# The mixer's pooled input: one matmul block over all 256 tokens with the channels on partitions, mapped in one go, and the output product started with the pooled channels

## The chip, the cores and the metric

The kernel runs on one core of a Trainium2 chip. The metric is the device time of one execution in microseconds (us); smaller is better. PE is TensorE (matmul), ACT is ScalarE, DVE is VectorE, POOL is GpSimd, SP is the engine whose queue issues the DMAs. The array of PE and its weight load overlap.

## What is computed

Two layers, each: a SwiGLU feed-forward part (FFN), a mixer, a second FFN, each followed by a residual sum and a layer norm. 256 tokens, 1024 channels. The mixer projects the input to 2560 channels: 512 for pooling (u) and 4 x 512 for a gated recurrence with four heads (q, f, v, g). The reference, cut to the pooling branch and the mixer's end:

```python
def multiscale_pool(u, pool_w, pool_scale):          # windows 2, 4, 8, 16 for four groups of 128 channels
    c = jnp.cumsum(u32, axis=1)
    for g, w in enumerate(POOL_WINDOWS):
        ...
        cnt = jnp.minimum(pos + 1, w)
        means.append((cg - lag) / cnt)
    pooled = jnp.stack(means, axis=2) - u32
    y = jnp.einsum('bsgc,gcd->bsgd', pooled, pool_w)
    return y.reshape(B, S, D_POOL) * pool_scale
...
h = x @ w_in[l]
y_pool = multiscale_pool(u, pool_w[l], pool_scale[l])
y_hgrn = head_rms_norm(hgrn2_recurrence(q, f_raw, v, lb), hgrn_norm_g[l]) * silu(g)
mix = concatenate([y_pool, y_hgrn]) @ w_out[l]
x = layer_norm(ALPHA * x + mix, ln_g[l, 1], ln_b[l, 1])
```

## The kernel before

**Numbers and products.** Every factor of a large product is split into a rounded part and its rest (`halves`, line 101: an ACT cast writes the high part, a DVE subtraction the low part), and a product is three matmuls (`mm3`, lines 95 to 99: high x high, high x low, low x high). In the projections of the mixer the stationary operand is a 128x128 piece of the transposed input `xt` and the moving one 512 columns of a weight. One `mm3` is one **slot**: it calls `later.tick()`, and work that was queued with `later(n, fn)` is written into the program n slots further on. PE's order is the order of this writing; ACT, DVE, POOL and SP take an order that a scheduler makes from priorities.

**Weights.** All weights come through one stream of 512 KB pieces (`Weight`, line 107): a DMA on SP's queue into one of five `raw` buffers, an ACT cast to `wh`, a DVE subtraction to `wl` (both at lines 102 and 103, 128x1024 elements), into a ring of eight pairs. A `raw` buffer is free for the next DMA when DVE's subtraction has read it; a pair in the ring is free when PE has made its last use of it (`used`).

**The mixer** (line 520) runs five projection blocks of 512 channels, each for two halves of 128 tokens, eight slots a half: f and q, then v, g and u. Each block has four weight pieces. Between the slots stand the decays (L634), the Gram matrices of the recurrence (L681, L686: `grams`), their product across the halves (L705, `cross`), the outputs per half (L722, L724: `output`), which DVE and POOL normalise into `y`, and the transposes of `y` (L740), eight slots after the outputs. u is made per half with the tokens on partitions: ACT copies it (L752), five slots later four transposes bring the channels onto partitions (L765), ACT copies them into `sum1` (L767), DVE makes the running sums for the windows (L773, L776, L777), nine slots later four matmuls apply `pool_w` (L783), and ACT and DVE scale and split the result into the operand of the output product (L787, L788). These matmuls with `pool_w` and those of the recurrence are full fp32, which PE runs as two passes, each with an instruction of its own.

**The output product** follows: for each half 16 slots over the eight pieces of `w_out`, in the order of `WOUT_ORDER`, which puts the recurrence's four pieces first. After a half comes its layer norm (lines 243 to 251 on DVE), and its transposes (L177) stand in the next half or the next FFN. The freed ring takes the first weights of that FFN.

Of the kernel before, what the change touches and what calls it, by code (L numbers as in the profile page):

```python
# [10 lines left out]
F32 = mybir.dt.float32  # L11
F32R = mybir.dt.float32r
U8 = mybir.dt.uint8
AF = mybir.ActivationFunctionType
# [17 lines left out]
M32, M8, S32 = 0, 96, 192  # L32
WINDOWS = (2, 4, 8, 16)
PAD = 16
WOUT_ORDER = (4, 5, 6, 7, 0, 1, 2, 3)
TINY = 2.0 ** -60
NEG = -1e30
RAW, NW, NX, ND = 5, 8, 2, 6
AHEAD, BEHIND = 100, 400
PINNED, STARTED = 4, 4  # L40
HT = 6
WARM = 17


# [30 lines left out]
def trunk(ctx: ExitStack, tc: tile.TileContext, t, out: bass.AP):  # L75
# [434 lines left out]
    class Mixer:  # L510
        def __init__(self, l):
            self.l = l
            self.win = [[Weight(t["win"][l, b, kq], "w", NW) for kq in range(4)] for b in range(NB)]
            self.wout = {kt: Weight(t["wout"][l, kt], "w", NW) for kt in WOUT_ORDER}

        def run(self):
            return mixer(self.l, self.win, self.wout)
# [1 line left out]
    def mixer(l, win, wout):  # L519
# [14 lines left out]
        def mixed(hf):  # L534

            if hf:
                mt[hf] = xth[:, place[0]], xtl[:, place[0]]
            else:
                mt[hf] = [xtp.tile([P, KT, P], F32R, name=n) for n in ("mth", "mtl")]
            return mt[hf]  # L540
# [177 lines left out]
        def output(hf):  # L718
            po = psa.tile([P, NH, P], F32, name="acc")
            for h in range(NH):  # L720
                hs = slice(h * P, (h + 1) * P)
                nc.tensor.matmul(po[:, h, :], Pm[hf][:, h, :], v[hf][:, hs], start=True, stop=hf == 0)  # L722
                if hf == 1:
                    nc.tensor.matmul(po[:, h, :], P01[0][:, h, :], v[0][:, hs], start=False, stop=True)  # L724
            sq = mp.tile([P, NH, P], F32, name="tB", bufs=2)
            nc.scalar.activation(sq, po, AF.Square)
            ms = sp.tile([P, NH], F32, name="ms")
            nc.vector.tensor_reduce(ms, sq, mybir.AxisListType.X, ALU.add)
            nc.vector.tensor_scalar(ms, ms, 1.0 / P, RMS_EPS, ALU.mult, ALU.add)
            nc.gpsimd.tensor_tensor(ms, ms, neghalf, ALU.pow)  # L730
            y = mp.tile([P, NH, P], F32, name="y", bufs=2)
            for h in range(NH):
                nc.vector.scalar_tensor_tensor(y[:, h, :], po[:, h, :], ms[:, h:h + 1],
                                               sg[hf][:, h * P:(h + 1) * P], ALU.mult, ALU.mult)

            def go():
                mixed(hf)
                pt = psg.tile([P, NH * P], F32, name="gu").rearrange("p (k t) -> p k t", k=NH)
                for h in range(NH):
                    nc.tensor.transpose(pt[:, h, :], y[:, h, :], ident)  # L740
                mh, ml = (m[:, 4:8, :] for m in mt[hf])
                nc.scalar.activation(mh, pt, AF.Copy, scale=gn[:, l:l + 1])
                nc.vector.scalar_tensor_tensor(ml, pt, gn[:, l:l + 1], mh.bitcast(F32), ALU.mult, ALU.subtract)
                ready[hf].add(1)
            later(8, go)

        ready = [set(), set()]
        sums = {}

        def post_u(hf, ps):  # L750
            un = mp.tile([P, 512], F32, name="u")
            nc.scalar.copy(un, ps)  # L752
            if hf == 0:
                for w in (1,) + WINDOWS[:-1]:
                    sums[w] = mp.tile([P, 4 if w < 4 else 6 - w.bit_length(), PAD + P], F32, name=f"sum{w}")

            def pooled():
                for w in sums:
                    if hf == 0:
                        nc.gpsimd.memset(sums[w][:, :, 0:PAD], 0.0)  # L760
                    else:
                        nc.gpsimd.tensor_copy(sums[w][:, :, 0:PAD], sums[w][:, :, P:P + PAD])
                pt = psg.tile([P, 4 * P], F32, name="gu").rearrange("p (k t) -> p k t", k=4)
                for g in range(4):
                    nc.tensor.transpose(pt[:, g, :], un[:, g * P:(g + 1) * P], ident)  # L765
                now = slice(PAD, PAD + P)
                nc.scalar.copy(sums[1][:, :, now], pt)  # L767
                pl = mp.tile([P, 4, P], F32, name="tB", bufs=2)
                for g, w in enumerate(WINDOWS):

                    half = sums[w // 2][:, -(4 - g):, :]
                    dst = sums[w][:, :, now] if w in sums else pl[:, g:g + 1, :]
                    nc.vector.tensor_tensor(dst, half[:, :, now], half[:, :, PAD - w // 2:PAD + P - w // 2], ALU.add)  # L773
                    mean = dst[:, 0, :]
                    if hf == 0:
                        nc.vector.tensor_tensor(mean[:, 0:PAD], mean[:, 0:PAD], fix[:, g, :], ALU.mult)  # L776
                    nc.vector.scalar_tensor_tensor(pl[:, g, :], mean, 1.0 / w, sums[1][:, g, now], ALU.mult, ALU.subtract)  # L777
                later(9, lambda: mapped(pl))

            def mapped(pl):  # L780
                py = psg.tile([P, 4 * P], F32, name="gu").rearrange("p (k t) -> p k t", k=4)
                for g in range(4):
                    nc.tensor.matmul(py[:, g, :], pw[:, g, :], pl[:, g, :], start=True, stop=True)  # L783
                for g in range(4):
                    mh, ml = (m[:, g, :] for m in mt[hf])
                    sc = pscale[:, l, g:g + 1]
                    nc.scalar.activation(mh, py[:, g, :], AF.Copy, scale=sc)  # L787
                    nc.vector.scalar_tensor_tensor(ml, py[:, g, :], sc, mh.bitcast(F32), ALU.mult, ALU.subtract)  # L788
                ready[hf].add(0)
            later(5, pooled)  # L790

        post_f(0, ps_f0)
        post_q(0, block(1, 0))
        post_f(1, block(0, 1))
        post_q(1, block(1, 1))
        for b, post in ((2, post_v), (3, post_g), (4, post_u)):
            for hf in range(2):
                ps = block(b, hf)
                if (b, hf) == (3, 0):
                    tc.keep_in_program_order(nc.scalar.preload_act_table_set("silu_and_others"))  # L800
                post(hf, ps)
        gb = load_gb(l, 1)
        for hf in range(2):
            if hf == 1:
# [1 line left out]
                guard.__exit__(None, None, None)  # L806
                guard = open_ffn()
            accs = [psa.tile([P, 512], F32, name="acc") for _ in range(2)]
            for n, kt in enumerate(WOUT_ORDER):
                later.wait(lambda: kt // 4 in ready[hf])  # L810
                wh, wl = wout[kt].parts
                for c in range(2):
                    cs = slice(c * 512, c * 512 + 512)
                    mm3(accs[c], mt[hf][0][:, kt, :], mt[hf][1][:, kt, :], wh[:, cs], wl[:, cs],
                        n == 0, n == KT - 1)
                wout[kt].used()
            if hf == 0:
                place.reverse()
# [43 lines left out]
def _layout(inputs):  # L862
# [3 lines left out]
        both = np.stack([gate, up], axis=2).reshape(DEPTH, KT // 2, 2, P, 2, NG, GW)  # L866
        return both.transpose(0, 5, 1, 3, 2, 4, 6).reshape(DEPTH, NG, KT // 2, P, ET)

    w_in = a["w_in"].reshape(DEPTH, KT // 2, 2, P, NB, 512)[:, :, :, :, [2, 1, 3, 4, 0]]
    cum, masks, fix = _constants()  # L870

    w0 = gu(a["ffn1_gate"], a["ffn1_up"])[0, 0].reshape(KT // 2, P, 2, 512).transpose(0, 2, 1, 3).reshape(KT, P, 512)
# [35 lines left out]
```

## Time and profile before

| | us |
|---|---|
| median of three runs (958.11 to 958.52) | 958.29 |
| time of the profiled execution | 958.23 |
| its span from first to last instruction | 956.5 |
| PE busy in the span | 946.6 |
| DVE busy | 654.8 |
| ACT busy | 519.6 |
| POOL busy | 32.4 |

Around the span lie 1.7 us. The page of the profile gives for each engine the time in which at least one of its instructions ran. Matmuls overlap on PE, so the duration of one is longer than the step from one start to the next; what a matmul costs is read from steps between starts in the timeline.

### The profile page before, as it was taken

The page shows a single profiled execution, that of the slowest core. Times are in us where ns is not written, and L with a number is a line of the kernel's source. Part 1 is how long each engine was busy: PE and PEld are TensorE (multiplying, and loading weights), DVE is VectorE, ACT ScalarE, POOL GpSimd, SP SyncE. Part 2 cuts the span into 40 slices and gives each one's busy share as a digit, 9 for nine tenths or more (in the row PEclk, how much of TensorE's full clock was granted, in tenths as well). Part 3 has the DMA queues.
Part 4 walks back from the last instruction along what each step waited for, and adds up shares of the span by engine and source line. Part 5 has one row for each costly group of instructions (what it writes and reads, how often), then busy time and mean ns, then how long its engine had stood idle before and what let it go on. Part 6 is the DMA issues. An engine that isn't in the chain of part 4 may idle for free. (4 is left out here: it accounts for less than half of the span.)

```text
span 956.5 us, 13129 instructions
## 1 busy us (share of the span) xinstructions
PE 946.6 (99%) x4817; PEld 800.0 (84%) x4817; DVE 654.8 (68%) x1104; ACT 519.6 (54%) x809; POOL 32.4 (3%) x50
## 2 busy tenths in 40 slices
PE   9999999999999999999999999999999999999996
PEld 7888888888887888888888888888888888888885
DVE  6875656679789765656676565557898896575625
ACT  6765454368456755444445645433985466546420
POOL 0000000001110000000000000000021000000000
PEclk9999999999999999999999999999999999999999
DMA  8977775332627876565346766552327377676301
GB/s 318 336 243 251 254 247 169 109 103 97 219 88 247 311 232 222 191 205 169 123 157 239 237 211 211 174 155 99 110 67 265 112 266 262 222 240 215 114 1 45
DMA packets 50801, 180.22 MB, mean 188 GB/s; under 512 B 6192, under 2 KB 6192, under 8 KB 50736
## 3 DMA queue, kind: packets, MB, share of 16 engines
q1 hardware_dynamic: 50544, 178.85, 55.5%
q8 instruction: 38, 0.62, 0.3%
q0 software_dynamic: 192, 0.53, 0.2%
q14 instruction: 27, 0.22, 0.1%
HBM read 178.30 MB, written 1.05 MB: 188 GB/s over the span
## 5 line engine op out<-in xcount | busy, mean ns | idle before, releaser
L102 ACT CAST wh<-raw 128x1024 fp32r<-128x1024 f32 x196 | 205.1, 1051 | 100.9 <-DMA raw<-in_gu 35.7
L103 DVE TENSOR_TENSOR wl<-raw,wh 128x1024 fp32r<-128x1024 f32 x196 | 235.9, 1219 | 27.0 <-PE gu L300 15.3
L300 PE MATMUL gu<-xt,wh 128*128 128x512 f32 x768 | 180.6, 391 | 0.0
L103 DVE TENSOR_TENSOR dl<-raw,dh 128x1024 fp32r<-128x1024 f32 x88 | 106.5, 1223 | 101.6 <-ACT dh L102 96.0
L300 PEld LDWEIGHTS gu<-xt,wh 128*128 128x128 f32 x768 | 144.1, 188 | 31.7
L102 ACT CAST dh<-raw 128x1024 fp32r<-128x1024 f32 x88 | 91.6, 1049 | 109.7 <-DMA raw<-in_dn 101.3
L96 PE MATMUL acc<-dh,hth 128*128 128x512 f32 x352 | 140.0, 398 | 0.1
L98 PE MATMUL acc<-dh,htl 128*128 128x512 f32 x352 | 138.1, 392 | 0.0
L97 PE MATMUL acc<-dl,hth 128*128 128x512 f32 x352 | 137.4, 390 | 0.0
L96 PE MATMUL gu<-wh,xt 128*128 128x512 f32 x320 | 128.7, 402 | 0.0
L98 PE MATMUL gu<-wh,xt 128*128 128x512 f32 x320 | 125.5, 392 | 0.0
L97 PE MATMUL gu<-wl,xt 128*128 128x512 f32 x320 | 125.0, 391 | 0.0
L300 PE MATMUL gu<-xt,wl 128*128 128x256 f32 x768 | 99.6, 282 | 0.0
L300 PEld LDWEIGHTS gu<-xt,wl 128*128 128x128 f32 x768 | 96.8, 191 | 1.9
L323 DVE TENSOR_TENSOR sil<-gu,sil 128x256 f32<-128x256 f32 x64 | 27.0, 422 | 83.7 <-ACT sil L322 83.7
L98 PEld LDWEIGHTS acc<-dh,htl 128*128 128x128 f32 x352 | 66.0, 188 | 14.8 <-DVE htl L103 0.2
L97 PEld LDWEIGHTS acc<-dl,hth 128*128 128x128 f32 x352 | 66.2, 188 | 12.7 <-DVE dl L103 0.3
L96 PEld LDWEIGHTS acc<-dh,hth 128*128 128x128 f32 x352 | 66.2, 188 | 12.5 <-ACT hth L102 0.5
L98 PEld LDWEIGHTS gu<-wh,xt 128*128 128x128 f32 x320 | 60.1, 188 | 13.1
L97 PEld LDWEIGHTS gu<-wl,xt 128*128 128x128 f32 x320 | 60.2, 188 | 11.4
L96 PEld LDWEIGHTS gu<-wh,xt 128*128 128x128 f32 x320 | 60.1, 188 | 11.0
L300 PE MATMUL gu<-xt,xh 128*128 128x512 f32 x256 | 62.4, 396 | 0.0
(182 smaller groups left out, 1056.2 us busy)
## 6 DMA issues: line engine op xcount, KB each, us to landing
raw<-in_gu SPq DMA_DIRECT2D x172, 512.0 KB, 4.4
raw<-in_dn SPq DMA_DIRECT2D x88, 512.0 KB, 4.6
raw<-in_win SPq DMA_DIRECT2D x40, 512.0 KB, 4.2
raw<-in_wout SPq DMA_DIRECT2D x16, 512.0 KB, 4.2
lng<-in_ln_g SPq DMA_DIRECT2D x6, 512.0 KB, 4.7
lnb<-in_ln_b SPq DMA_DIRECT2D x6, 512.0 KB, 6.0
raw<-in_first SPq DMA_DIRECT2D x5, 384.0 KB, 5.7
x<-in_first SPq DMA_DIRECT2D x3, 384.0 KB, 7.2
```

The source lines that it names most:

```text
L96: nc.tensor.matmul(ps, lh, wh, start=start, stop=False)
L97: nc.tensor.matmul(ps, lh, wl, start=False, stop=False)
L98: nc.tensor.matmul(ps, ll, wh, start=False, stop=stop)
L102: first = nc.scalar.copy(dst_h, src)
L103: return first, nc.vector.tensor_tensor(dst_l, src, dst_h.bitcast(F32), ALU.subtract)
L300: nc.tensor.matmul(ps[i][part][:, 2 * S - w:], weight.parts[lo][:, c:c + P], x[:, 0:w], start=kt == 0 and not lo, stop=kt == KT - 1 and lo ...
L323: nc.vector.tensor_tensor(dst, p[:, 0:S], dst, ALU.add)
```

## The change

The blocks of u and g change places: in the rearranged `w_in` u is now block 3 and g block 4. The projection of u is no longer made per half. `pooled_input` runs it once for all 256 tokens with the weight as the stationary operand (128 channels at a time) and the input as the moving one (256 tokens), so that the channels lie on partitions from the start: 8 x 4 x 3 matmuls of 256 columns; six of them count as a slot. ACT copies the two results into one set of running sums for all tokens, which takes the buffers of the decays (`EA`, `EB`), DVE makes the sums at once, and twelve slots later `mapped` applies `pool_w` to 256 tokens at a time and writes the operands of both halves. The output product takes the pieces of `w_out` in their natural order, the pooled channels first.

```diff
-WOUT_ORDER = (4, 5, 6, 7, 0, 1, 2, 3)
+MAPPED = 12
...
             def go():
-                mixed(hf)
                 pt = psg.tile([P, NH * P], F32, name="gu").rearrange("p (k t) -> p k t", k=NH)
...
-        def post_u(hf, ps):
-            un = mp.tile([P, 512], F32, name="u")
-            nc.scalar.copy(un, ps)
...
+        def pooled_input():
+            ps = [psg.tile([P, 2, S], F32, name="gu") for _ in range(2)]
+            for kt in range(KT):
+                later.wait(lambda: min(xT[0].done, xT[1].done) > kt)
+                weight = win[3][kt // 2]
+                xh, xl = (xt2[:, kt, n].rearrange("p h t -> p (h t)") for n in range(2))
+                for i in range(4):
+                    c = (kt % 2) * 512 + i * P
+                    wh, wl = (part[:, c:c + P] for part in weight.parts)
+                    for n, (w, x) in enumerate(((wh, xh), (wh, xl), (wl, xh))):
+                        nc.tensor.matmul(ps[i // 2][:, i % 2, :], w, x,
+                                         start=kt == 0 and n == 0 and i % 2 == 0,
+                                         stop=kt == KT - 1 and n == 2 and i % 2 == 1)
+                    if i % 2:
+                        later.tick()
+                if kt % 2:
+                    weight.uses = 1
+                    weight.used()
+            sums = {w: mp.tile([P, 4 if w < 4 else 6 - w.bit_length(), PAD + S], F32, name="EA" if w < 4 else "EB", bufs=2)
+                    for w in (1,) + WINDOWS[:-1]}
+            for w in sums:
+                nc.gpsimd.memset(sums[w][:, :, 0:PAD], 0.0)
+            for i, p in enumerate(ps):
+                for hf in range(2):
+                    nc.scalar.copy(sums[1][:, 2 * i:2 * i + 2, PAD + hf * P:PAD + hf * P + P],
+                                   p[:, :, place[hf] * P:place[hf] * P + P])
+            pl = mp.tile([P, 4, S], F32, name="pl")
+            now = slice(PAD, PAD + S)
+            for g, w in enumerate(WINDOWS):
+                half = sums[w // 2][:, -(4 - g):, :]
+                dst = sums[w][:, :, now] if w in sums else pl[:, g:g + 1, :]
+                nc.vector.tensor_tensor(dst, half[:, :, now], half[:, :, PAD - w // 2:PAD + S - w // 2], ALU.add)
+                mean = dst[:, 0, :]
+                nc.vector.tensor_tensor(mean[:, 0:PAD], mean[:, 0:PAD], fix[:, g, :], ALU.mult)
+                nc.vector.scalar_tensor_tensor(pl[:, g, :], mean, 1.0 / w, sums[1][:, g, now], ALU.mult, ALU.subtract)
+            later(MAPPED, lambda: mapped(pl))
+
+        def mapped(pl):
+            py = [psg.tile([P, 2, S], F32, name="gu") for _ in range(2)]
+            for g in range(4):
+                nc.tensor.matmul(py[g // 2][:, g % 2, :], pw[:, g, :], pl[:, g, :], start=True, stop=True)
+            for hf in range(2):
+                mixed(hf)
                 for g in range(4):
...
-        for b, post in ((2, post_v), (3, post_g), (4, post_u)):
...
+        for hf in range(2):
+            post_v(hf, block(2, hf))
+        pooled_input()
+        for hf in range(2):
+            ps = block(4, hf)
...
-    w_in = a["w_in"].reshape(DEPTH, KT // 2, 2, P, NB, 512)[:, :, :, :, [2, 1, 3, 4, 0]]
+    w_in = a["w_in"].reshape(DEPTH, KT // 2, 2, P, NB, 512)[:, :, :, :, [2, 1, 3, 0, 4]]
```

Three places show what moves. The first is PE's queue in layer 0 around the matmuls with `pool_w`. Before, inside the first half's output product (`acc<-wh,mth`), transposes and mapping of the two halves of u stand apart:

```order
L765 MATMUL gu<-ident,u 128x128 x4
L96 MATMUL acc<-wh,mth 128x512
L97 MATMUL acc<-wl,mth 128x512
L98 MATMUL acc<-wh,mtl 128x512
L783 MATMUL gu<-tB,pw 128x128 x4
L96 MATMUL acc<-wh,mth 128x512
```

Now, in the second half of the g block (`gu<-wh,xt`), ahead of the first half's outputs (L722):

```order
L791 MATMUL gu<-pl,pw 128x256 x4
L96 MATMUL gu<-wh,xt 128x512
L97 MATMUL gu<-wl,xt 128x512
L98 MATMUL gu<-wh,xt 128x512
L722 MATMUL acc<-v,Pm 128x128 x4
```

The transposes are gone, and one mapping with columns twice as wide takes the place of two, a slot ahead of the outputs L722, instead of after them.

The second place is ACT's queue in layer 1, after the last copies of `grams` (L690); `wh<-raw` are the casts of `w_out`. Before:

```order
L690 COPY Pm<-acc 32x2x32 x2
L102 CAST wh<-raw 128x1024 [waits DMAHW6_49,DVE_49]
L726 ACTIVATE tB<-acc 128x512 [waits PE_49]
L102 CAST wh<-raw 128x1024 [waits DMAHW7_49,DVE_49,PE_49]
L715 ACTIVATE sg<-gu 128x512 [waits PE_49]
L102 CAST wh<-raw 128x1024 [waits DMAHW0_49,DVE_49,Activation_49]
L707 COPY P_6955<-acc 128x512 [waits PE_49]
```

Now:

```order
L690 COPY Pm<-acc 32x2x32 x2
L102 CAST wh<-raw 128x1024 [waits DMAHW6_49,DVE_49]
L102 CAST wh<-raw 128x1024 [waits DMAHW7_49,DVE_49]
L774 COPY EA<-gu 128x2x128 [waits DVE_49,PE_49]
L774 COPY EA<-gu 128x2x128
L102 CAST wh<-raw 128x1024 [waits DMAHW0_49,PE_49]
L774 COPY EA<-gu 128x2x128 [waits PE_49]
L707 COPY P_7003<-acc 128x512 [waits PE_49]
L774 COPY EA<-gu 128x2x128
```

The four copies of u into the running sums (L774) stand among the same three casts, the last two behind the cast that waits for the third of these pieces.

The third place is DVE's queue in layer 1 where the running sums begin; `wl<-raw,wh` are the subtractions of `w_out`. Before, the sums of the first half (L773) come after the recurrence's part of the operand (L743):

```order
L103 TENSOR_TENSOR wl<-raw,wh 128x1024 [waits DMAHW1_49,Activation_49]
L103 TENSOR_TENSOR wl<-raw,wh 128x1024 [waits DMAHW2_49,Activation_49]
L743 SCALAR_TENSOR_TENSOR xt<-gu,gn,xt 128x4x128 [waits Activation_49]
L773 TENSOR_TENSOR sum_7022<-sum_7021 128x4x128 [waits Activation_49]
L103 TENSOR_TENSOR wl<-raw,wh 128x1024 [waits DMAHW3_49,Activation_49]
L776 TENSOR_TENSOR sum_7022<-sum_7022,fix 128x16 [waits DVE_49]
```

Now they come right behind the masked copies of `grams` (L698, L700):

```order
L103 TENSOR_TENSOR wl<-raw,wh 128x1024 [waits DMAHW7_49,Activation_49]
L698 COPY_PREDICATED Pm<-masks,acc 128x32x2 [waits DVE_49]
L782 TENSOR_TENSOR EA<-EA 128x4x256 [waits Activation_49,Pool_49]
L700 COPY_PREDICATED Pm<-masks,acc 128x128 [waits DVE_49]
L784 TENSOR_TENSOR EA<-EA,fix 128x16 [waits DVE_49]
L782 TENSOR_TENSOR EB<-EA 128x3x256 [waits Pool_49]
L785 SCALAR_TENSOR_TENSOR pl<-EA 128x256 [waits DVE_49]
```

The sums of all tokens are one chain, ahead of the outputs' reduction and ahead of the subtractions of the last four `w_out` pieces.

## Rows read from the trace of the kernel before

**Rows 1.** The page: busy time of each engine in us, its share of the span, its instructions.

```profile
PE 946.6 (99%) x4817; PEld 800.0 (84%) x4817; DVE 654.8 (68%) x1104; ACT 519.6 (54%) x809; POOL 32.4 (3%) x50
```

**Rows 2.** Sums by stretch of the mixer of layer 1: us from the span's start, length, busy time of PE, PE's weight load, DVE, ACT and POOL with counts, PE clock, share of DMA, GB/s. The stretch begins with the g block.

```profile
705.78:721.17 15.39, 15.36 (x84) 13.23 (x83) 15.39 (x48) 12.47 (x21) 2.68 (x2) 1.00 0.50 165
```

**Rows 3.** PE's timeline in layer 0, two slots of a projection, three apart: start, duration, line, tiles, form, count.

```profile
251.24 0.40 PE L96 MATMUL gu<-wh,xt 128*128 128x512 f32 x1
...
253.30 0.39 PE L96 MATMUL gu<-wh,xt 128*128 128x512 f32 x1
```

**Rows 4.** PE's timeline in an FFN: first of four runs of eight matmuls with 256 columns, and what follows the fourth.

```profile
331.12 1.10 PE L300 MATMUL gu<-xt,xl 128*128 128x256 f32 x8
...
334.91 0.40 PE L96 MATMUL acc<-dh,hth 128*128 128x512 f32 x1
```

**Rows 5.** PE's timeline in the first half's output product of layer 0, around the second transposes of u and the first mapping.

```profile
269.39 0.60 PE L765 MATMUL gu<-ident,u 128*128 128x128 f32 x4
269.75 0.47 PE L96 MATMUL acc<-wh,mth 128*128 128x512 f32 x1
...
270.52 1.05 PE L783 MATMUL gu<-tB,pw 128*128 128x128 f32 x8
271.33 0.47 PE L96 MATMUL acc<-wh,mth 128*128 128x512 f32 x1
...
272.10 0.40 PE L96 MATMUL acc<-wh,mth 128*128 128x512 f32 x1
```

**Rows 6.** Groups of PE by line and form: fp32 matmuls of 256 and of 128 columns (count of passes, busy us, mean ns of one, idle time before).

```profile
L686 PE MATMUL acc<-EB,EA 128*128 128x256 f32 x32 | 8.4, 385 | 0.0
...
L783 PE MATMUL gu<-tB,pw 128*128 128x128 f32 x32 | 4.2, 275 | 0.0
```

**Rows 7.** PE's timeline in the output products, layer 0 and layer 1: first matmuls of two consecutive slots.

```profile
272.80 0.40 PE L96 MATMUL acc<-wh,mth 128*128 128x512 f32 x1
...
273.66 0.39 PE L96 MATMUL acc<-wh,mth 128*128 128x512 f32 x1
...
745.09 0.40 PE L96 MATMUL acc<-wh,mth 128*128 128x512 f32 x1
...
745.96 0.40 PE L96 MATMUL acc<-wh,mth 128*128 128x512 f32 x1
```

**Rows 8.** PE's timeline in layer 1: the Gram matmuls of the second half, first and second pair of heads, and where the g block is after the product across the halves.

```profile
713.15 1.68 PE L686 MATMUL acc<-EB,EA 128*128 128x192 f32 x8
...
718.58 1.95 PE L686 MATMUL acc<-EB,EA 128*128 128x192 f32 x8
...
724.14 0.48 PE L96 MATMUL gu<-wh,xt 128*128 128x512 f32 x1
```

**Rows 9.** DVE's timeline in layer 0: the running sums of the first half (512, then 384 columns) around a weight subtraction of 1024 columns.

```profile
265.49 0.68 DVE L773 TENSOR_TENSOR sum<-sum 128x512 f32<-128x512 f32 x1
266.09 1.22 DVE L103 TENSOR_TENSOR wl<-raw,wh 128x1024 fp32r<-128x1024 f32 x1
267.23 0.21 DVE L776 TENSOR_TENSOR sum<-sum,fix 128x16 f32<-128x16 f32 x1
267.36 0.54 DVE L773 TENSOR_TENSOR sum<-sum 128x384 f32<-128x384 f32 x1
267.83 0.28 DVE L777 SCALAR_TENSOR_TENSOR tB<-sum,sum 128x128 f32<-128x128 f32 x1
```

**Rows 10.** ACT's timeline in layer 1: two casts of `w_out`, and in brackets the idle time before and what ended it.

```profile
722.62 1.05 ACT L102 CAST wh<-raw 128x1024 fp32r<-128x1024 f32 x1 [0.57 <-DMA raw<-in_wout]
...
724.63 1.05 ACT L102 CAST wh<-raw 128x1024 fp32r<-128x1024 f32 x1 [0.46 <-DMA raw<-in_wout]
```

**Rows 11.** The first half's outputs on their way to `y`: ACT and DVE in layer 0, then DVE and POOL in layer 1.

```profile
250.06 0.60 ACT L726 ACTIVATE tB<-acc 128x512 f32<-128x512 f32 x1 [0.77 <-PE acc L722]
...
252.72 1.13 DVE L733 SCALAR_TENSOR_TENSOR y<-acc,ms,sg 128x128 f32<-128x128 f32 x4 [1.14 <-POOL ms L730]
...
723.03 1.21 DVE L103 TENSOR_TENSOR wl<-raw,wh 128x1024 fp32r<-128x1024 f32 x1
...
723.20 1.92 POOL L730 TENSOR_TENSOR ms<-ms,neghalf 128x4 f32<-128x4 f32 x1 [6.63 <-DVE ms L729]
```

**Rows 12.** DVE's timeline in layer 0: the layer norm of the first half, among the last split of the pooled operand (L788), and the first subtractions for the next FFN.

```profile
278.60 0.35 DVE L788 SCALAR_TENSOR_TENSOR xt<-gu,pscale,xt 128x128 fp32r<-128x128 f32 x1 [2.96 <-ACT xt L787]
278.90 0.69 DVE L243 SCALAR_TENSOR_TENSOR x<-acc,x 128x512 f32<-128x512 f32 x1
...
285.15 4.62 DVE L103 TENSOR_TENSOR wl<-raw,wh 128x1024 fp32r<-128x1024 f32 x4
```

**Rows 13.** PE's timeline in the second FFN of layer 0 and of layer 1: two places where a matmul starts late.

```profile
302.54 0.40 PE L98 MATMUL gu<-wh,xt 128*128 128x512 f32 x1
303.03 0.50 PE L96 MATMUL acc<-dh,hth 128*128 128x512 f32 x1
...
792.24 0.39 PE L98 MATMUL acc<-dh,htl 128*128 128x512 f32 x1
792.78 0.44 PE L406 MATMUL gu<-ident,hn 128*128 128x128 f32 x2 [0.15 <-DVE hn L334]
```

**Rows 14.** The chain of work that ended last, pieces of it ahead of the second of these places (start, us, what).

```profile
764.47 4.72 DMA raw<-in_dn
769.21 1.05 ACT dh L102
```

More of the change, by code (lines that the diff above doesn't have):

```diff
@@ L513, in __init__ @@
             self.win = [[Weight(t["win"][l, b, kq], "w", NW) for kq in range(4)] for b in range(NB)]
-            self.wout = {kt: Weight(t["wout"][l, kt], "w", NW) for kt in WOUT_ORDER}
+            self.wout = {kt: Weight(t["wout"][l, kt], "w", NW) for kt in range(KT)}
         def run(self):
@@ L747, in mixer @@
         ready = [set(), set()]
-        sums = {}
-        def post_u(hf, ps):
-            un = mp.tile([P, 512], F32, name="u")
-            nc.scalar.copy(un, ps)
[L753 to L783, printed above, removed]
@@ L784, in mapped @@
+        def mapped(pl):
[4 more added lines that the diff above has]
+                mixed(hf)
                 for g in range(4):
                     mh, ml = (m[:, g, :] for m in mt[hf])
-                    sc = pscale[:, l, g:g + 1]
-                    nc.scalar.activation(mh, py[:, g, :], AF.Copy, scale=sc)
@@ L788, in mapped @@
-                    nc.vector.scalar_tensor_tensor(ml, py[:, g, :], sc, mh.bitcast(F32), ALU.mult, ALU.subtract)
+                    src, sc = py[g // 2][:, g % 2, hf * P:hf * P + P], pscale[:, l, g:g + 1]
+                    nc.scalar.activation(mh, src, AF.Copy, scale=sc)
+                    nc.vector.scalar_tensor_tensor(ml, src, sc, mh.bitcast(F32), ALU.mult, ALU.subtract)
                 ready[hf].add(0)
-            later(5, pooled)
         post_f(0, ps_f0)
@@ L795, in mixer @@
         post_q(1, block(1, 1))
-        for b, post in ((2, post_v), (3, post_g), (4, post_u)):
[L797 to L801, printed above, removed]
+        for hf in range(2):
[3 more added lines that the diff above has]
+            ps = block(4, hf)
+            if hf == 0:
+                tc.keep_in_program_order(nc.scalar.preload_act_table_set("silu_and_others"))
+            post_g(hf, ps)
         gb = load_gb(l, 1)
@@ L808, in mixer @@
             accs = [psa.tile([P, 512], F32, name="acc") for _ in range(2)]
-            for n, kt in enumerate(WOUT_ORDER):
+            for kt in range(KT):
                 later.wait(lambda: kt // 4 in ready[hf])
@@ L814, in mixer @@
                     mm3(accs[c], mt[hf][0][:, kt, :], mt[hf][1][:, kt, :], wh[:, cs], wl[:, cs],
-                        n == 0, n == KT - 1)
+                        kt == 0, kt == KT - 1)
                 wout[kt].used()
```

## The prediction

> **What bounds the kernel now.** I read the profile's page first: PE has an instruction running in 946.6 of 956.5 us [rows 1], so the end is set by PE's steps and by the places where PE waits, and a change is worth what it takes from or adds to these. Next I read the sums by stretch: in layer 1, where the new running sums will have to be made, DVE is busy in all of the 15.39 us of the stretch [rows 2]; there is no slack for work that PE waits for. Then PE's timeline, where a price is a step from start to start, because durations overlap.
>
> **The block of u.** Three slots of a projection start 2.06 us apart, from 251.24 to 253.30 [rows 3], so a slot takes 0.687 us, and today's two halves of eight slots 10.99 us a layer. The new form, weights stationary and 256 columns moving, stands in the FFN: 32 such matmuls from 331.12 to 334.91, 3.79 us [rows 4], 0.118 us each. The block needs 8 x 4 x 3 = 96 of them, 11.37 us: 0.38 us more a layer, **+0.76** in all. The columns are the same in number; the added weight loads show as a 256-column step that is longer than half of the 512-column step (0.118 against 0.687/6 = 0.1145).
>
> The Trainium skill ("TensorE: Matmul & The Clock Gate", Back-to-back issue gap) gives for an isolated gap the columns over 2.4 GHz and 2.5 ns, so 109 and 216 ns; as an estimate from that section of the Trainium skill the block would cost 0.1 us a layer more instead of 0.38, and the sum would fall by a further 0.5 us. The rows are longer at both widths, so I go by them.
>
> **The transposes.** A group of four takes 0.36 us to the next start, and the slot behind it is 0.77 instead of 0.687 long [rows 5]: 0.443 us. Four groups go: **-1.77**. ACT's copies around them go too; PE waited for none of them.
>
> **The mapping.** Eight passes of 128 columns take 0.81 us plus the same 0.083 [rows 5], 0.112 a pass. A pass of 256 columns lasts 385 ns, one of 128 columns 275 [rows 6]; 110 more, so its step is at most 0.222, and eight of them 1.78 us against 2 x 0.893 now. **0**, within 0.1 either way.
>
> **Waits that go.** In each layer's output product one slot is 0.86 or 0.87 us long instead of 0.687 [rows 7]: the low part of the pooled operand (L788) comes late there. Now the mapping stands a slot, the outputs (L722) and three slots ahead of the product: **-0.35**. In layer 1 the second Gram group takes 1.95 us against 1.68 for the first [rows 8]; it needs accumulators that DVE's masked copies (L698) free, and DVE stood in a weight subtraction ahead of them. In the new queue the first masked copy stands ahead of that subtraction. I take all of it, **-0.27**; the bound is 0 if DVE is late all the same.
>
> **The running sums.** A step of DVE is 0.60 us for 512 columns, 1.14 for 1024, 0.13 for 16 and 0.47 for 384 [rows 9]; on that line 768 take 0.87 and 256 take 0.34. The chain for 256 tokens is 1024, 768, 512 and 256 columns of sums, four corrections of 16 and four last steps of 256: 1.14 + 0.87 + 0.60 + 0.34 + 4 x 0.13 + 4 x 0.34 = 4.83 us. PE reaches the last quarter of the mapping 12 slots and three quarters after the block, 8.24 + 3 x 0.444 = 9.6 us.
>
> In layer 0 there stand in between: a cast of 1.05, two copies (about 0.3 each), a subtraction of 1.14 and the chain, 7.7 us with handovers. Covered by 1.9 us.
>
> In layer 1 it is closer. The casts of `w_out` wait for their DMAs; the third of them on ACT's queue starts at 724.63, when its piece has landed [rows 10]. The buffers for these pieces are freed by the same subtractions as now, so I keep that time. In the new queue the last two copies of u stand behind that cast, with the copy L707 between: 724.63 + 1.05 + 0.3 + 0.5 + 0.35 = 726.8. Then the chain, with a masked copy (0.25) and one subtraction (1.14) among its steps, to 733.0. PE: now, after the 16 slots that begin at 705.78, the decays, the Gram matrices, one output and the product across the halves, it is at 724.14 [rows 8]. The output moves out (eight passes, 0.89), the wait of 0.27 goes, the block is 0.38 longer: 723.4. Twelve slots and three quarters later it wants the last quarter, at 732.9. Late by **0.1**.
>
> Behind this chain on DVE wait two more subtractions (to 735.3) and the first two splits (L798, to 735.8); ACT's next two L797 wait for those, and L726, which leads to `y`, waits behind them, to 736.4 (PE's outputs are done at 735.2). From L726 to the end of `y` it takes 3.79 us (250.06 to 253.85), and with a subtraction beside it POOL's step took 1.92 us [rows 11] instead of the 1.1 that lie between here. That gives 741.1 to 741.5; PE wants the last part of `y` eight slots and three transposes after the outputs, at 741.0. Late by about **0.4**. I take **+0.5** for both; the bounds are 0 and 1.5, since a landing 1 us later moves the whole chain by as much.
>
> **Waits of the next FFN.** After each mixer one matmul of the second FFN starts late: a step of 0.49 where 0.229 is usual, and one of 0.54 [rows 13], 0.57 us in all. The chain that ended last runs to the second of these through the FFN's DMAs and casts [rows 14], whose buffers DVE's first subtractions free. Those start at 285.15, after the first half's layer norm, which began at 278.90 among the splits L788 [rows 12]; four of them, 0.26 us each, delay it. Now these splits are long done, so the chain starts up to 1 us earlier against PE. Bounds 0 and -0.57; the chain crosses DMA landings that I can't follow, so I take half, **-0.28**.
>
> **Sum.** 0.76 - 1.77 - 0.35 - 0.27 + 0.5 - 0.28 = -1.41. Against the profiled execution's own 958.23 (1.7 us around its span, unchanged) this gives 956.8; that execution lies 0.06 below the median of the three runs, which changes nothing.
>
> **Rivals.** *The waits go altogether.* The FFN's waits vanish whole and the chains in layer 1 are just in time: 956.8 - 0.29 - 0.5 = 956.0. For it: the layer norm gains more than those waits are long. Against: DVE's full stretch in layer 1.
>
> *Half the columns cost half.* If the weight load hides wholly behind 256 columns, the block costs what it does now, and the sum is 0.76 lower: 956.1. The gap formula of the Trainium skill, named above, points this way too. Against: 32 matmuls in a row took 0.118 us each, and nothing in the new block is kinder.
>
> *New waits eat the gain.* DVE comes to the sums 1.4 us later than I have it in layer 1; PE then waits at the mapping or at `y`, not both, because a wait at the first moves the second too: 958.2. For it: 15.39 of 15.39 us. Against: one table load and several copies leave ACT.
>
> *Slower.* The copies of u stand behind a cast that waits for a DMA, in PE's path by way of the mapping, where today nothing of u waits for `w_out`. Its price is one for one once the copies in layer 1 end after 726.7; to pass 960.2 they would have to end 3.4 us later, after 730.1, which takes a landing 3.4 us later than now or a layer 0 whose 1.9 us of cover is gone too. 960.6 then. Against: the pieces are issued by the same subtractions in the same order.
>
> **How the numbers follow.** What a measurement of this kernel can tell from no change is about 0.2%, 1.9 us: faster is below 956.4, slower above 960.2. Chances: forecast 0.50 (its own range 956.0 to 957.7), all waits gone 0.22, half cost 0.05, gain eaten 0.15, slower 0.08. A quarter of the forecast lies below 956.4, so faster is 0.22 + 0.05 + 0.12 = 0.39, the same 0.53, slower 0.08. The range leaves out the slower case and the far end of the two faster ones: 955.4 to 958.8.
>
> **What would show it.** Steps of the 256-column matmuls of the block near 0.118 us; none of the slots of the output product at 0.86; the mapping in layer 0 without idle time before it; in layer 1 its last quarter and the transposes of `y` at most some tenths late, with DVE as releaser; the steps of 0.49 and 0.54 in the second FFNs shorter or gone. The forecast is wrong if the mapping in layer 1 waits over 1 us, if layer 0 waits at all, or if a place that I priced at nothing (the Gram matrices, the output product's second half, the next FFN's first weights) shows a new wait.

## The result and the profile after

The changed kernel took 959.75 us (median of 21 runs, 958.1 to 961.9), the kernel before 958.29 in as many runs beside it: a ratio of 1.0012, interval 1.0006 to 1.0017. It is slower by 0.06 to 0.17%. The forecast was 956.8 with 955.4 to 958.8, so the time lies outside the range, on the other side of no change. A part of that isn't in the span: over the 21 runs the time less the span is 2.0 us on the mean, and 1.8 in the kernel before (its runs beside the experiments).

The first trace of the changed kernel is of one of its shorter executions, 958.32 us with a span of 956.6; a second one, taken with the experiments (`again`), is of 960.01 with 957.9. Both are used.

The page's busy times of the changed kernel, answering to [rows 1]:

```profile
PE 944.6 (99%) x4881; PEld 802.9 (84%) x4881; DVE 653.2 (68%) x1088; ACT 514.3 (54%) x808; POOL 27.6 (3%) x42
```

PE is busy 2.0 us less, and the span is not shorter. To see where it went I took the end-to-end step of each matmul in the trace (the first from the span's start) and called what it has over the usual step of its form, where that is more than 0.1 us, a wait. Before: 944.7 us of steps and 4.2 of waits. After: 943.3 and 5.5; in the second trace 943.4 and 6.7. So **PE's own work did fall by 1.3 to 1.4 us**, and waits took 1.3 to 2.4 us in its place. The list of PE's waits names them. Its columns are the waiter, what it waited for, us in total, times, longest. First the kernel before, then after:

```profile
PE gu L406 <- DVE hn L334: 0.4, 2, 0.3
```

```profile
PE gu L406 <- DVE hn L334: 1.8, 3, 0.9
...
PE gu L791 <- DVE pl L785: 0.7, 1, 0.7
```

The second, at the mapping, is in the forecast's sum, if too small. The first is not in the mixer at all: L406 are the FFN's transposes of a gate's product `hn`. Two of the three times are in the FFNs behind the mixers, at 319.6 and 792.7 us; the third, at 506 us, is in layer 1's first FFN, where the kernel before waits too.

**The block of u.** PE's timeline in the block of layer 0, three matmuls to a group of weights:

```profile
235.79 0.28 PE L760 MATMUL gu<-xt,wl 128*128 128x256 f32 x1
235.91 0.40 PE L760 MATMUL gu<-xt,wh 128*128 128x256 f32 x2
236.15 0.28 PE L760 MATMUL gu<-xt,wl 128*128 128x256 f32 x1
```

Three steps in 0.36 us, 0.12 each. All 192 steps sum to 22.98 us, 0.1197 each; the 96 matmuls of 512 columns that they replace (32 slots of three) took about 96 x 0.229 = 21.98.

**Places with a wait less.** PE's output product of layer 0, first matmuls of consecutive slots, and the second Gram group of layer 1:

```profile
271.70 0.40 PE L96 MATMUL acc<-wh,mth 128*128 128x512 f32 x1
272.40 0.39 PE L96 MATMUL acc<-wh,mth 128*128 128x512 f32 x1
273.08 0.39 PE L96 MATMUL acc<-wh,mth 128*128 128x512 f32 x1
```

```profile
718.19 1.68 PE L686 MATMUL acc<-EB,EA 128*128 128x192 f32 x8
```

No slot of 0.86 us as in [rows 7], and 1.68 us where [rows 8] has 1.95.

**The mapping in layer 1.** PE's timeline; then what it waited for, on ACT and on DVE:

```profile
731.38 1.03 PE L791 MATMUL gu<-pl,pw 128*128 128x256 f32 x4
733.07 0.70 PE L791 MATMUL gu<-pl,pw 128*128 128x256 f32 x2 [0.66 <-DVE pl L785]
```

```profile
724.76 1.06 ACT L102 CAST wh<-raw 128x1024 fp32r<-128x1024 f32 x1 [0.54 <-DMA raw<-in_wout]
725.73 0.36 ACT L774 COPY EA<-gu 128x256 f32<-128x256 f32 x1
725.99 0.58 ACT L707 COPY P<-acc 128x512 f32<-128x512 f32 x1
726.46 0.38 ACT L774 COPY EA<-gu 128x256 f32<-128x256 f32 x1
```

```profile
726.95 1.23 DVE L782 TENSOR_TENSOR EA<-EA 128x1024 f32<-128x1024 f32 x1 [1.34 <-ACT EA L774]
...
731.46 1.22 DVE L103 TENSOR_TENSOR wl<-raw,wh 128x1024 fp32r<-128x1024 f32 x1
732.59 0.42 DVE L785 SCALAR_TENSOR_TENSOR pl<-pl,EA 128x256 f32<-128x256 f32 x1
```

The copies end at 726.84 and the sums at 733.01, within 0.1 us of what the prediction worked out (726.8 and 733.0). PE wanted the last quarter at 732.25 and not at 732.9, because it was ahead: it came into the mixer of layer 1 0.9 us earlier than in the kernel before. In the second trace it came in no earlier; there DVE was late, with the copies done at 727.53 and the sums at 733.69, and PE wanted the last quarter at 733.23.

**The gate behind the mixer of layer 1.** PE's timeline at the wait of 792.7, then ACT and DVE ahead of it, in the changed kernel:

```profile
791.45 0.39 PE L98 MATMUL acc<-dh,htl 128*128 128x512 f32 x1
792.73 0.44 PE L406 MATMUL gu<-ident,hn 128*128 128x128 f32 x2 [0.89 <-DVE hn L334]
```

```profile
789.78 1.05 ACT L102 CAST dh<-raw 128x1024 fp32r<-128x1024 f32 x1
790.74 0.38 ACT L333 ACTIVATE sil<-gu 128x256 f32<-128x256 f32 x1
```

```profile
791.12 1.22 DVE L103 TENSOR_TENSOR dl<-raw,dh 128x1024 fp32r<-128x1024 f32 x1
792.25 0.41 DVE L334 TENSOR_TENSOR hn<-sil,gu 128x256 f32<-128x256 f32 x1
```

The gate (`sil` on ACT, `hn` on DVE) stands behind a `w_down` piece in both queues. The same place in the kernel before ([rows 13], 792.78):

```profile
790.05 1.05 ACT L102 CAST wh<-raw 128x1024 fp32r<-128x1024 f32 x1
791.01 0.38 ACT L333 ACTIVATE sil<-gu 128x256 f32<-128x256 f32 x1
```

```profile
791.18 1.22 DVE L103 TENSOR_TENSOR wl<-raw,wh 128x1024 fp32r<-128x1024 f32 x1
792.31 0.41 DVE L334 TENSOR_TENSOR hn<-sil,gu 128x256 f32<-128x256 f32 x1
```

There too one piece stands directly ahead of it, but an earlier one, `wh`. So `hn` starts at the same time in both (792.25 and 792.31), while PE is there 0.8 us earlier now (its last matmul ahead of the transposes starts at 791.45, before at 792.24). In the built program one can count: ACT has 110 weight casts ahead of this gate in layer 0 and 270 in layer 1 before, **111 and 271** after, and DVE's subtractions likewise. The gate ahead of it has one more as well, 107 for 106 and 267 for 266. ACT's queue in the FFN behind the mixer of layer 0 up to that gate, the program before:

```
L333 ACTIVATE sil<-gu 128x256
L102 CAST wh<-raw 128x1024 x3
L102 CAST hth<-gu 128x256
L102 CAST wh<-raw 128x1024
L333 ACTIVATE sil<-gu 128x256
L102 CAST dh<-raw 128x1024 x2
```

and after:

```
L333 ACTIVATE sil<-gu 128x256
L102 CAST wh<-raw 128x1024 x3
L102 CAST hth<-gu 128x256
L102 CAST dh<-raw 128x1024
L333 ACTIVATE sil<-gu 128x256
L102 CAST dh<-raw 128x1024
```

The diff touches no line of the FFN. The order of ACT and DVE is made for the whole program when it is built, and with other work in the mixer it comes out otherwise behind it. That is what the experiments test.

### The profile page after: what moved, and what is told of

Same layout as the page of the kernel before. It is cut to its first block, busy times and chain, and to the rows that moved or that the text cites. A ratio compares the mean times of both kernels' runs of the same rounds, so it can differ in the third digit from the quotient of the medians.

```text
span 956.6 us, 13230 instructions
## 1 busy us (share of the span) xinstructions
PE 944.6 (99%) x4881; PEld 802.9 (84%) x4881; DVE 653.2 (68%) x1088; ACT 514.3 (54%) x808; POOL 27.6 (3%) x42
## 3 DMA queue, kind: packets, MB, share of 16 engines
HBM read 178.30 MB, written 1.05 MB: 187 GB/s over the span
## 5 line engine op out<-in xcount | busy, mean ns | idle before, releaser
L96 PE MATMUL gu<-wh,xt 128*128 128x512 f32 x288 | 115.5, 401 | 0.0
L98 PE MATMUL gu<-wh,xt 128*128 128x512 f32 x288 | 112.7, 391 | 0.0
L97 PE MATMUL gu<-wl,xt 128*128 128x512 f32 x288 | 112.5, 391 | 0.0
L98 PEld LDWEIGHTS gu<-wh,xt 128*128 128x128 f32 x288 | 54.1, 188 | 11.7
L97 PEld LDWEIGHTS gu<-wl,xt 128*128 128x128 f32 x288 | 54.2, 188 | 10.3
L96 PEld LDWEIGHTS gu<-wh,xt 128*128 128x128 f32 x288 | 54.1, 188 | 10.1
```

Of the source, the lines that this page charges most:

```text
L96: nc.tensor.matmul(ps, lh, wh, start=start, stop=False)
L97: nc.tensor.matmul(ps, lh, wl, start=False, stop=False)
L98: nc.tensor.matmul(ps, ll, wh, start=False, stop=stop)
```

## Experiments

In the diffs `...` stands for lines left out. Each kernel is compared with the kernel before on the same chip. The ratio behind a median is an estimate from all runs and need not be the quotient of the two medians; its 95% interval stands in brackets.

**1. The changed kernel again.** No edit.

> The changed kernel, unaltered, for a second trace beside the first and for a common yardstick. Its profiled execution was about as long as that of the kernel before, while its median lay 1.5 us above: if the new wait of 0.92 us at the mapping of layer 1 is the place that varies from execution to execution, this trace shows another length there; if the weights' supply of the FFNs is what varies, it shows the steps at the first transposes after the third and the tenth gate block (319.6 and 792.7 us in the first trace, 0.60 and 1.1 us late) with other lengths and the mapping alike.

959.47 us, 1.0004 of before (0.9993 to 1.0015). The wait at the mapping was 0.51 us (0.82 in the first trace, by start-to-start steps less the usual one), those at the gates 1.31 and 0.81 (0.54 and 1.04). Both vary, the gates more. Their sum is only 0.2 us above that of the first trace; the 1.7 us by which this execution is longer come from other places too, among them 0.55 at the gate ahead of that of layer 1 (788.79), 0.8 at a wait at 101 us, ahead of both mixers, and 0.4 outside the span. By its own interval the repeat can't be told from the kernel before; that the kernel is slower rests on the 21 runs above.

**2 and 3. One layer at a time.**

```diff
+NEW = (0,)          # and (1,)
...
+        if l in NEW:
             (blocks, pooled_input, mapping and w_out's order of the changed kernel)
+        else:
+            (those of the kernel before)
```

> The new form in layer 0 alone, layer 1 as in the kernel before. Theory A (the loss is layer 1's: its sums stand behind w_out's casts and subtractions and PE waits at the mapping): 957.5, 0.8 below before, the sum of layer 0's terms 0.38 - 0.885 - 0.175 - 0.14. Theory B (whatever a mixer saves is given back in the FFN behind it, because its weights do not come sooner): 958.3, no change, with PE ahead by about 1.3 us at the end of the mixer and the lead lost at the FFN's transposes. Theory C (the new form itself costs more than summed): above 958.8.

> The new form in layer 1 alone, layer 0 as in the kernel before. Theory A: 959.5 to 960, all of the loss and some more, with a wait of 0.9 us or more at the mapping. Theory B: 958.3 to 959, a smaller wait at the mapping in the sum, and the lead at the end of the mixer lost at the FFN's transposes. The two single-layer changes add up to the change of both, within 0.5 us, if the layers are independent.

Layer 0 alone: 959.73 us, 1.0011 (1.0001 to 1.0020). Layer 1 alone: 958.68, 0.9996 (0.9987 to 1.0005). **Theory A falls**: the layer in which the mapping waits for nothing makes the kernel slower, and the layer with the wait doesn't. The two differences add up to about that of the changed kernel. By the number alone theory C fits, but the time isn't lost in the new form: PE's own steps sum to 0.5 us less than before, the mixer of layer 0 has no new wait, and the gate behind it has the longest of that place in all traces:

```profile
320.52 0.44 PE L408 MATMUL gu<-ident,hn 128*128 128x128 f32 x2 [1.59 <-DVE hn L336]
```

Layer 1 has its wait at the mapping (0.74) and at its gate (0.57), but it also loses the wait in the Gram matrices. That wait is 0.27 us in [rows 8] and 0.17, 0.71, 0.89 and 0.94 in the four other traces with the old form in layer 1 (end to end), and no trace with the new form has it.

**4. PE's work taken out.** Of the kernel before, with all its casts, subtractions and DMAs; DVE's order is otherwise in three splits of the mixers.

```diff
+            if lean and 1 <= kt <= 4:
+                nc.tensor.matmul(ps, xt.h[:, kt, :], wh[:, cs], start=False, stop=False)
+                nc.tensor.matmul(ps, xt.l[:, kt, :], wh[:, cs], start=False, stop=False)
+                later.tick()
+            else:
                 mm3(...)
```

> The kernel before with 16 matmuls of 512 columns a layer... that is, of each of the two halves' blocks of u in both layers the product with the low part of the weights is left out for four of eight row blocks (the output lacks that product): 16 matmuls x 0.229 = 3.66 us of TensorE alone, spread as 1.83 a layer, with all casts, subtractions and DMAs kept. If what PE saves in a mixer reaches the end, 954.6. Theory B: clearly less arrives, 956.5 or above, and the trace shows longer waits at the transposes of the FFNs behind the mixers.

(It is eight matmuls a layer, 16 in all.) 954.44 us, 0.9951 (0.9938 to 0.9964): 4.3 us less, all of the 3.66 and perhaps more. **Theory B falls** as the main cause: a PE that is 1.8 us ahead at the end of a mixer is not stopped by late weights. Its gates have 110 and 270 casts ahead, and neither made PE wait. (At the gate of layer 1's first FFN, 506 us, it waits 1.08, the longest of that place in all traces.)

**5 and 6. The gate's place, forward and back.** In the changed kernel the piece is loaded in the program after the gate and kept behind it; in the kernel before the gate (`made`) is kept behind that piece.

```diff
+HELD = (114, 274)
...
-            while position[0] < len(stream) and stream[position[0]].load():
+            while position[0] < len(stream) and position[0] != hold[0] and stream[position[0]].load():
...
+            if (g, hf) == (1, 1) and not self.mixer_next:
...
+                hold[0], pinned[0], released[0] = position[0] + 1, 1, True
+                advance()
...
```

```diff
...
+            if (g, hf) == (1, 1) and not self.mixer_next:
+                for ins, ahead in zip(made, stream[(114 if self.ln[0] == 0 else 274)].pair_of):
+                    tc.add_manual_dep(ins.ins, ahead.ins.name, mybir.DependencyInfo(
...
```

The first is `a_gate`, the second `b_gate`; in the traces each differs from its kernel in the order of ACT and DVE at these two gates and nowhere else.

> The changed kernel, but in the FFN behind each mixer the second half's gate of group 1 stands ahead of one w_down piece's cast and subtraction again (110 and 270 weight casts ahead of it, as in the kernel before, where the changed kernel has 111 and 271); nothing else differs. Theory D (the changed kernel's static order put one more weight piece ahead of that gate, on ACT and on DVE, and PE's transposes wait for it): the wait there, 0.6 to 1.8 us behind layer 0 and 0.6 to 1.1 behind layer 1 in the traces with the new form, falls to 0.3 or less at each, and the median is 1.2 to 2 us below the changed kernel's, near 958. Theory B (the weights themselves come too late for a PE that is ahead): the wait moves to the next product, and the median stays at the changed kernel's.

> The kernel before, with the opposite swap: the same gate in both layers stands behind one more w_down piece (111 and 271). Theory D: 0.7 to 1.5 us above the kernel before, with new waits at the two FFNs' transposes behind the mixers. Theory B: no change, since PE is no earlier here than before.

`a_gate`: 957.86 us, 0.9993 (0.9985 to 1.0002), 1.6 to 1.9 below the two medians of the changed kernel and 1.1 to 1.8 by the ratios; its interval lies clear of that of the 21 runs and overlaps that of the repeat. `b_gate`: 961.25, 1.0031 (1.0019 to 1.0043), 2.7 above the kernel before. One cast and one subtraction in each layer, moved past one gate, make and unmake the loss; **theory D holds**, and the price in `b_gate` is higher than I expected. One thing didn't come as expected: the wait at layer 1's gate is gone in `a_gate`, but that of layer 0 was 0.67 in its trace, not 0.3 or less. The gate behind layer 1 in `a_gate`, on ACT and then on PE (no idle time in brackets):

```profile
788.68 0.36 ACT L103 CAST hth<-gu 128x256 fp32r<-128x256 f32 x1
788.94 0.39 ACT L335 ACTIVATE sil<-gu 128x256 f32<-128x256 f32 x1
789.22 2.03 ACT L103 CAST dh<-raw 128x1024 fp32r<-128x1024 f32 x2
```

```profile
791.25 0.39 PE L99 MATMUL acc<-dh,htl 128*128 128x512 f32 x1
791.48 0.38 PE L414 MATMUL gu<-ident,hn 128*128 128x128 f32 x2
```

And in `b_gate`, ACT, DVE, PE:

```profile
793.10 1.05 ACT L102 CAST wh<-raw 128x1024 fp32r<-128x1024 f32 x1 [0.64 <-DMA raw<-in_gu]
794.35 1.05 ACT L102 CAST dh<-raw 128x1024 fp32r<-128x1024 f32 x1 [0.20 <-DMA raw<-in_dn]
795.31 0.37 ACT L333 ACTIVATE sil<-gu 128x256 f32<-128x256 f32 x1
```

```profile
795.43 1.22 DVE L103 TENSOR_TENSOR dl<-raw,dh 128x1024 fp32r<-128x1024 f32 x1
796.58 0.41 DVE L334 TENSOR_TENSOR hn<-sil,gu 128x256 f32<-128x256 f32 x1
```

```profile
797.04 0.44 PE L410 MATMUL gu<-ident,hn 128*128 128x128 f32 x2 [1.58 <-DVE hn L334]
```

The cast's own row says what the gate waited for: the piece's DMA. ACT starts the cast when it has landed, the gate's activation stands behind, DVE's subtraction of the same piece stands ahead of `hn`, and PE's transposes come last. In the changed kernel's first trace the cast ahead of the gate (789.78) starts without idle time, so there the place in the queues was enough.

**7 and 8. The sums ahead of a subtraction in layer 1**, alone and with the gates.

```diff
+            with tc.high_priority(offset=100):
                 for g, w in enumerate(WINDOWS):
                     ...
```

> The changed kernel with the running sums of layer 1 ahead in DVE's queue of the one weight subtraction that stood among them and of two masked copies; layer 0, ACT, PE and the gates are untouched. If that subtraction (1.15 us) is what makes PE wait 0.6 to 0.9 us at the mapping's last quarter: no wait there, and 0.6 to 0.9 us below the changed kernel, unless the FFN behind waits longer for the gate (theory D), which would take most of it back. If the copies behind w_out's cast decide alone, the wait stays.

> Both repairs of the changed kernel at once, the gates' order and the sums ahead. By theory D with the wait at the mapping: what the prediction's sum gave without its new waits, 956.2 to 957, 1.3 to 2 us below the kernel before. If something not yet seen eats the gain, 958 or above.

`a_sums`: 959.58 us, 1.0008 (0.9999 to 1.0017). No wait at the mapping, no gain. PE's timeline at the transposes of `y`:

```profile
740.50 0.39 PE L98 MATMUL acc<-wh,mtl 128*128 128x512 f32 x1
740.96 1.10 PE L739 MATMUL gu<-ident,y 128*128 128x128 f32 x4
741.90 0.39 PE L722 MATMUL acc<-v,Pm 128*128 128x128 f32 x2
```

Four transposes take 0.94 us to the next start here where they take 0.44 otherwise, and the first comes 0.46 after the matmul ahead, not 0.23: each waits for its quarter of `y`, 0.7 us in all. The wait moved. `a_both`: 957.64, 0.9995 (0.9986 to 1.0005), as `a_gate` within what the runs can tell, and not the 956.2 to 957 of my expectation; 0.6 us of waits at `y`.

**9 and 10. The gate of layer 1's first FFN**, which waits in every trace up to here (0.1 to 1.1 us; 0.41 before), ahead of two pieces: in the changed kernel with both repairs and u's last copies ahead of the third cast, and in the kernel before.

```diff
-HELD = (114, 274)
+HELD = (114, 180, 274)
...
-            if (g, hf) == (1, 1) and not self.mixer_next:
+            if (g, hf) == (1, 1) and not self.first:
...
```

> The changed kernel with the gates behind both mixers ahead of the extra weight piece (as in a_gate), the same gate of layer 1's first FFN ahead of two such pieces (176 instead of 178 casts; the trace of the kernel before waits 0.47 us there, the other traces 0.16 to 1.15), and in layer 1 the last two copies of u ahead of w_out's third cast and the sums ahead of two subtractions. If the gates and the chain of layer 1 are all that stood between the prediction's sum and the run: 956.0 to 956.8, without waits at the mapping or at the gate of 506 us. If the waits only move on to the transposes of y and to the next gates: 957.5, as a_both.

> The kernel before with the gate of layer 1's first FFN ahead of the same two pieces (176 instead of 178), its gates behind the mixers in their old order. If that gate's order costs what its wait shows: 958.0 to 958.3, 0.3 to 0.6 below the kernel before. Against a_best it shows what the change of the mixer itself is worth when the gates stand alike: by the prediction's sum 1.4 us, by the theory that the new waits of the mixer eat it 0 to 0.5.

957.65 (0.9992, 0.9983 to 1.0001) and 957.81 (0.9992, 0.9983 to 1.0001). That wait is gone in both. With like gates the two forms of the mixer are equal here within what the runs can tell; but `a_best` pays more at `y`, as copies and sums now delay the subtractions and what is behind them:

```profile
740.99 1.10 PE L748 MATMUL gu<-ident,y 128*128 128x128 f32 x4 [1.11 <-DVE y L742]
```

**11 and 12. The mapping one slot later on PE alone.**

```diff
-MAPPED = 12
+MAPPED = 13
```

> a_gate with the mapping one slot later in PE's order (slot 13 instead of 12, both layers); ACT's, DVE's and the queues' orders are the same. The slot is 0.69 us, and in a_gate PE waited 0.97 us for the last quarter in layer 1. If that wait is by itself a loss: 0.3 us of it left and 0.7 us below a_gate, near 957.2. If what follows the mapping on ACT and DVE is the bound (their splits and y), the wait turns up at the transposes of y or at the output product, and the median stays at a_gate's 957.9.

> a_map13 and the gate of layer 1's first FFN ahead of two weight pieces, as in a_best and b_best, where the wait at 506 us was gone. If the gains add: 0.4 to 0.6 us below a_map13, 956.7 or so, 1.5 to 2 us below the kernel before. If waits of one place are made up at the next, no better than a_map13.

`a_map13`: 958.64, 0.9999 (0.9991 to 1.0008): not better than `a_gate`. The wait at the mapping fell to 0.2 us, and 0.7 came up at `y`. `a_final13` (the same, and layer 1's first gate ahead of two pieces): **956.92, 0.9986 (0.9977 to 0.9995)**, the one version that computes everything and is faster than the kernel before beyond its interval; it is the best of six repaired versions, so some of that can be chance. As the lone difference between the two is worth 0.4 to 0.7 us by the wait it removes, some of the 1.7 us between their medians is spread of the runs.

The waits at the two gates in all fourteen traces (us, start to start less the usual 0.23):

| weight casts ahead of the gate | traces | waits | mean |
|---|---|---|---|
| layer 0: 110 | 9 | 0 to 0.77 | 0.33 |
| layer 0: 111 | 5 | 0.54 to 1.75 | 1.10 |
| layer 1: 270 | 9 | 0 to 0.31 | 0.05 |
| layer 1: 271 | 5 | 0.57 to 1.74 | 0.96 |

The two differences sum to 1.7 us, about what `a_gate` gained. Like compared with like, the layers with the new form wait 0.63 us less on the mean at layer 0's gate with one piece fewer ahead and 0.77 less at layer 1's (1.4 together; `a_gate` gained 1.1 to 1.9), those with the old form 0.85 and 1.63 (2.5, with `b_gate` as the only trace with the piece more; it lost 2.7). The count isn't all of it in layer 0: with 110 casts ahead the old form waits 0.11 there (four traces), the new one 0.51 (five). So some 0.4 us of waiting there comes with the new mixer of layer 0 and not with the piece; why was not tested.

## Why the prediction was wrong, step by step

**Waits of the next FFN: the step that failed.** I had -0.28, with bounds 0 and -0.57, because the subtractions behind the layer norm would start earlier. They did, by 1.4 to 1.8 us in layer 0, and the late step of [rows 13] at 303 us is gone from both traces. (A smaller one behind it, at 304.62 and 0.23 end to end, is gone from the first and 0.21 in the second; it is in none of the sums.) But I took the queues of the FFN to be as before, and looked no further than the mixer for what had moved. At the two gates PE waits 1.58 us in the first trace, 2.12 and another 0.55 at a gate nearby in the second, against 0.31 before. Against the 0.57 of before the term is 1.58 - 0.57 = +1.0 in the first trace and 2.12 + 0.55 - 0.57 = +2.1 in the second. With their mean in place of -0.28 the sum is +0.4, and with the next three corrections (0.3, 0 to 0.23, and 0.2) +0.9 to +1.2; measured were +1.2 by the ratio and +1.5 by the medians. The row that would have warned me was among my own: [rows 13] has 792.78 waiting for `hn`, and I read it as the chain of `w_down`'s DMA and cast in [rows 14] without asking which piece stands ahead of the gate.

**The running sums: the right place, too small.** +0.5, in two parts of 0.1 and 0.4; measured 0.92 in the first trace and, counted like that, 0.6 to 1.8 in the others with the new form in layer 1 (0.8 on the mean of the three whose queues are the changed kernel's there). In the first trace and these three all of it but 0.1 is at the mapping, not at `y`. The 0.4 for `y` doesn't even follow from its terms: 736.4 + 3.79 + 0.82 = 741.0, just when PE wants it. So it is luck that +0.5 came as near as it did. In the first trace DVE's chain ended where I had it and PE came earlier; in the second the chain ended 0.7 us later than I had it. What I had as "not both" holds in part: freed at the mapping, the wait comes back at `y` (`a_sums`, `a_both`), but `a_map13` and `a_final13` wait at both (0.2 and 0.8, 0.4 and 0.8 end to end).

**The block: 0 to 0.23 too cheap.** 0.1197 us a step against the 0.118 of [rows 4], so +0.99 instead of +0.76 at 0.229 a step of the old form. But the old steps aren't all alike: over the whole trace the steps of all products into `gu` with weights, the FFNs' included, sum to 0.7 us more than before, so this correction isn't firm. The gap formula of the Trainium skill ("TensorE: Matmul & The Clock Gate", Back-to-back issue gap), which is for an isolated matmul, would have had +0.2 as an estimate. This trace disagrees with it at 256 columns, with weights changed ahead of every matmul, by 0.011 us a step.

**Around the span: 0.2 missed.** I kept the 1.7 us of one execution as unchanged. On the mean of the runs it is 1.8 before and 2.0 after (1.8 to 2.1 in the repaired versions); why was not traced.

**The transposes, the mapping's work, the slots, the Gram wait: right.** The first are gone; a pass of the mapping takes 0.216 us (0.222 at most, I had said); the slots are 0.69; the Gram group 1.68. Layer 0's mapping waits for nothing. PE's own steps fell by 1.3 to 1.4 us, where 0.76 - 1.77 = -1.01 was forecast; the loss is in the waits and, by 0.2, outside the span.

**The rivals.** "New waits eat the gain" was nearest in mechanism, with the wrong place and, at 958.2, too low a price: it puts them in layer 1's mixer, and the runs put most of them into the FFNs. "Slower" needed copies after 730.1; they ended at 726.84, so the kernel was slower by another way than the one I had priced.

Open: how much the mixer's new form is worth with like gates. Five pairs of medians say -0.5 to 0.9 us, each within its uncertainty (`a_best` and `b_best` in one comparison 0.2; against the kernel before `a_gate` 0.6, `a_both` 0.9, `a_map13` -0.5; `a_final13` against `b_best`, in different ones, 0.9). By the mean spans the same pairs say 0.1 to 1.2. Why the built order comes out one piece further on was not traced.

## What to carry to other kernels

Where one scheduler orders the whole program, compare the queues behind the changed stage too, not only in it: count, for each instruction that PE will wait for, how many transfers' casts stand ahead of it, before and after. One more can cost more than the edit saves. A wait that is removed in a stretch where an engine is full can come back at that engine's next product, as it did here at `y`; test the pair and not the one.

## What the runs showed of the hardware that I had not expected

One cast of 1.05 us and one subtraction of 1.22 moved past one gate in each layer cost 2.7 us in the median (`b_gate`), 1.35 a gate: more than either takes alone, less than the two in a row. In layer 1 the gate there also waits for a DMA that lands 1.25 us after that of the piece ahead (the two casts of `b_gate`, 793.10 and 794.35, both released by their DMA). And 3.66 us of PE's work brought 4.3 (3.5 to 5.9 by the interval), so nothing beside PE held the time at its old length.
